# Sums of the weight tiles by transfers that add, and another order of the seven products, in a hybrid-decoder layer

## The chip, the cores and the metric

The kernel runs on one core of a Trainium2 chip. A core has five engines with queues of their own: TensorE (PE, matmuls; its weight loads are shown apart as PEld), VectorE (DVE), ScalarE (ACT), GpSimd (POOL) and SyncE (SP). Each works through its own instructions strictly in order. Transfers are issued on SP's queue (plain ones) and on POOL's (here: those that add what they carry to what lies at their destination). The metric is the device time of one execution, in microseconds; lower is better.

## The reference

One layer on x of 1024 rows by 1024 columns, float32: a norm, a pooling mixer (four causal windows of 2, 4, 8 and 16 rows, a 256x256 matrix for each quarter of the columns), a residual, and a gated ConvFFN, which holds most of the work:

```python
def conv_ffn(x, w_in, conv_w, conv_b, w_out):          # x: 1024 x 1024
    h = causal_depthwise_conv(x @ w_in, conv_w, conv_b)  # w_in: 1024 x 5632
    val, gate = jnp.split(h, 2, axis=-1)
    return (jax.nn.silu(gate) * val) @ w_out             # w_out: 2816 x 1024

x = x + pool_mixer(rms_norm(x, norm_mix_g), pool_w, pool_b, pool_scale)
x = x + conv_ffn(rms_norm(x, norm_ffn_g), ffn_w_in, ffn_conv_w, ffn_conv_b, ffn_w_out)
```

## The kernel before

**Stages.** The mixer comes first (to about 75 us), eight blocks of 128 rows one behind the other. Then the product with w_in, in 22 tiles of 128 + 128 hidden columns (a val and a gate block), to about 468 us, and the product with w_out (the line with `oP`), which fills the rest.

**A tile of w_in.** A tile is one load of 1 MB (`load_in`, SP, tile `win`, two buffers). It holds four quarters, A11, A12, A21 and A22, each 128x512. The normed activations are held as operands of their own: B11, B21, B22 and the combinations T1 to T4. A tile's product is made in seven products and not eight (Winograd's form of Strassen's method), and for that four sums of quarters are needed: S3 = A11 + A21, S1 = A21 + A22 (written over A21), S2 = A11 + S1 (over A11), S4 = A12 + S2 (over A12). The table `STEPS` says which left operand meets which right one, and in which PSUM bank: P1 A11 B11 in X, P6 S2 T2 in Y, P5 S1 T1 in Z, P2 A12 B21 in X, P7 S3 T3 in Y, P3 S4 B22 in Z, P4 A22 T4 in Y. P2 adds onto P1's bank, P3 onto P5's, P7 and P4 onto P6's, and between two products of one bank an engine reads what stands there (`step`): after P1 ScalarE (q1), after P6 VectorE (q2, in the profile `q<-Y`), after P5 VectorE (r), after P7 VectorE (hb).

**A product.** Every left operand is split in a high part (ScalarE's copy, rounded) and the rest (VectorE's subtraction): `split`, named A11s, S1s and so on, seven buffers (`hl`). A product is twelve matmuls of 128x512.

**The end of a tile.** Three-tap convolution of val and gate (ScalarE one wide instruction, VectorE two, for each), Silu on ScalarE, VectorE's product, a store of 512 KB on SP (`g_dram`). It is done by the engines while TensorE is at the next tile.

**What sets the order.** A list `events` of (tile, product) gives TensorE's order; the first two tiles are interleaved with the mixer. At each event the operand of the event five further on is prepared (`prep_in`): its sums, then its split. When a tile's A22 has been prepared, the load of the tile after next is issued into the buffer that it leaves. A list scheduler then merges the engines' streams; what it made of them is shown below.

**Where the sums are made.** For tiles 0 and 1 by transfers: `sums_in` with step 0 loads A11 a second time from memory into a buffer of its own for S3 (SP, 256 KB) and issues two adding transfers of 256 KB on POOL's queue (S3 += A21, then A21 += A22); with step 1 two more (A11 += S1, then A12 += S2). For tiles 2 to 21 `prep_in` makes all four by VectorE, in the helper `add` (line 353 in the profile, `win<-win` and `S<-win`).

**The norm's factors.** `gain_rows` spreads the 1024 factors of the second norm over all partitions with eight matmuls against an identity. The constant `ident` holds its rows turned (even ones first); `woven` reads it with a step of 64, so that the result stands in plain order.

Of the kernel before, what the change touches and what calls it, by code (L numbers as in the profile page):

```python
# [10 lines left out]
AF = mybir.ActivationFunctionType  # L11
# [3 lines left out]
P = 128  # L15
# [4 lines left out]
NK = D // P  # L20
NF = F // P
# [6 lines left out]
FOLD = 2 * D**0.5  # L28
# [22 lines left out]
def woven(t):  # L51
    return t.rearrange("p (a b) -> p b a", a=2)
# [11 lines left out]
def trunk_kernel(ctx: ExitStack, tc: tile.TileContext, x, consts, par, rows, pool_w, w_in, w_out, out):  # L64
    nc = tc.nc
# [14 lines left out]
    def bank2(name):  # L80
        return ps_p.tile([P, 2 * NH], F32, tag="ps", name=name)

    def raw_tile(name):
        return work.tile([P, 2, D], F32, tag="raw", name=name, bufs=2)

    def hl_tile(name):
        return hls.tile([P, 2, NH], F32R, tag="hl", name=name, bufs=7)

    def split(src, name, log=None):
        t = hl_tile(name)  # L90
        nc.scalar.activation(t[:, 0, :], src, AF.Copy)  # L91
        m = nc.vector.tensor_tensor(t[:, 1, :], src, t[:, 0, :].bitcast(F32), ALU.subtract)  # L92
        if log is not None:
            log.append(m.ins)
        return t
# [20 lines left out]
    scale = rows_raw[:, 0, :GRP]  # L116
# [49 lines left out]
    ident = cst[:, ID:]  # L166

    marks = {}
# [27 lines left out]
    def mixer_norm(j):  # L196
        t = bands[j] = pp.tile([P, NG, P], F32, tag="bandr", name=f"bandr{j}", bufs=2)
        for groups in [slice(0, 2), slice(2, 4)] if j == 0 else [slice(0, NG)]:
            marks[f"band{j}"] = normed(t[:, groups, :], (band if j else band0)[:, groups, :], stats[j])
# [46 lines left out]
    def gain_rows():  # L246
        ps = bank2("ps_gain")
        for k in range(NK):
            gain = par_sb[:, GF + k : GF + k + 1].to_broadcast([P, P])
            marks["gain_pe"] = nc.tensor.matmul(ps[:, k * P : (k + 1) * P], gain, woven(ident), start=True, stop=True).ins  # L250
        gain_b = pp.tile([P, D], F32, tag="gain_b", name="gain_b")
        marks["gain"] = nc.scalar.activation(gain_b, ps, AF.Copy, scale=FOLD).ins
        return gain_b

    ds, gains = {}, []
# [6 lines left out]
    def mixer_window(j, ps=None):  # L262
        ps = window_sums(j) if ps is None else ps
        dh = ds[j] = pp.tile([P, NK, P], F32, tag="dh", name=f"dh{j}", bufs=2)
        ps3 = ps.rearrange("p (c s) -> p c s", c=NK)
        first = ps3[:, :, :HALO]
        if j == 0:
            marks["first"] = nc.vector.tensor_tensor(first, first, fac, ALU.mult).ins
        elif j > 1:
            nc.vector.tensor_tensor(first, first, edges[:, :, j * HALO : (j + 1) * HALO], ALU.add)  # L270
        marks[f"dh{j}"] = nc.scalar.activation(dh, ps3, AF.Copy).ins
# [9 lines left out]
    def mixer_out(j, stats=True):  # L281
        dh = ds.pop(j)
        ps = bank2(f"psy{j}")
        for c in range(NK):
            o = ps[:, c // 2 * GRP : (c // 2 + 1) * GRP]
            nc.tensor.matmul(o, dh[:, c, :], wps[:, c, :], start=c % 4 == 0, stop=False, skip_group_check=True)  # L286
        for h in range(2):
            cols = slice(h * NH, (h + 1) * NH)
            m = nc.tensor.matmul(ps[:, cols], ones, bias_hl[:, cols], start=False, stop=True, skip_group_check=True)
        marks[f"psy{j}"] = m.ins  # L290
        x1 = n2s[j] = xs.pop(j)
        marks[j] = nc.vector.tensor_tensor(x1, ps, x1, ALU.add).ins
        nc.sync.dma_start(x1_dram[j * P : (j + 1) * P, :], x1)
        if stats:
            mixer_out_stats(j)
# [4 lines left out]
    def ffn_norm(j):  # L300
        x1, r = n2s[j]
        n2 = n2s[j] = pp.tile([P, D], F32, tag="n2", name=f"n2_{j}", bufs=2)
        nc.vector.tensor_tensor(r[1], r[0], r[1], ALU.mult)
        nc.vector.scalar_tensor_tensor(n2, x1, r[1], gains[0], op0=ALU.mult, op1=ALU.mult)
# [40 lines left out]
    def load_in(n):  # L345
        raws[n] = raw_tile(f"win{n}")
        nc.sync.dma_start(raws[n], w_in[order[n]])
# [4 lines left out]
    def add(out, a, b):  # L352
        nc.vector.tensor_tensor(out, a, b, ALU.add)  # L353

    def tmp(name):
        return work.tile([P, NH], F32, tag="sum", name=name, bufs=3)

    def sums_in(n, step):

        def more(out, a):  # L360
            nc.gpsimd.dma_start(out, a, accum_op=ALU.add)

        a11, a12, a21, a22 = (raws[n][:, i, k * NH : (k + 1) * NH] for i in range(2) for k in range(2))
        if step == 0:
            s3 = sums[n, "S3"] = tmp(f"S3_{n}")
            nc.sync.dma_start(s3, w_in[order[n]][:, 0, :NH])
            more(s3, a21)
            more(a21, a22)
        else:
            sums[n, "S2"] = a11  # L370
            more(a11, a21)
            sums[n, "S4"] = a12
            more(a12, a11)

    def prep_in(n, op):
        a11, a12, a21, a22 = (raws[n][:, i, k * NH : (k + 1) * NH] for i in range(2) for k in range(2))
        if op in ("S1", "S2") and (n, "S3") not in sums:
            s3 = sums[n, "S3"] = tmp(f"S3_{n}")
            add(s3, a11, a21)
            add(a21, a21, a22)  # L380
        if op in ("S2", "S4") and (n, "S2") not in sums:
            sums[n, "S2"] = a11
            add(a11, a21, a11)
        if op == "S4" and (n, "S4") not in sums:
            add(a12, a12, a11)
        if op == "S3":
            src = sums[n, "S3"]
        else:
            src = {"A11": a11, "A12": a12, "S1": a21, "A22": a22, "S2": a11, "S4": a12}[op]
        aops[n, op] = split(src, f"{op}s_{n}")  # L390
        if op == "A22" and n + 2 < NF:
            load_in(n + 2)

    def product(bank, a, b, opens):
        m = 0
        for k in range(4):
            ks = slice(k * P, (k + 1) * P)
            for i, l in ((0, 0), (0, 1), (1, 0)):
                nc.tensor.matmul(bank, a[:, i, ks], woven(b[:, l, k, :]), start=opens and m == 0, stop=m == 11, skip_group_check=not opens)  # L399
                m += 1  # L400

    STEPS = {
        "P1": ("A11", "B11", "X"), "P6": ("S2", "T2", "Y"), "P5": ("S1", "T1", "Z"), "P2": ("A12", "B21", "X"),
        "P7": ("S3", "T3", "Y"), "P3": ("S4", "B22", "Z"), "P4": ("A22", "T4", "Y"),
    }
# [54 lines left out]

    events = [(n, p) for p in ("P1", "P2") for n in range(2)]
    events += [(n, p) for p in ("P5", "P3") for n in range(2)] + [(n, p) for n in range(2) for p in ("P6", "P7", "P4")]
    events += [(n, p) for n in range(2, NF) for p in STEPS]
    LOOK = 5

    def prep_event(k):
        if k < len(events):
            n, p = events[k]
            prep_in(n, STEPS[p][0])

    def event(k):
        if k >= 4:
            prep_event(k + LOOK)
        n, p = events[k]
        step(n, p)
        if p == "P4":
            gated(n)
# [44 lines left out]
    for j in range(2, NS + 4):  # L522
        if 3 < j < NS:
            mixer_norm(j)
        if 1 <= j - 1 < NS and j > 2:
            mixer_window(j - 1, {3: sums2, 4: sums3}.get(j))
        if 1 <= j - 2 < NS:
            with tc.issue_after(marks[f"band{min(j, 4)}"]) if j > 2 else nullcontext(), tc.issue_after(marks["psd3"]):
                mixer_out(j - 2)
        if 0 <= j - 2 < NS:  # L530
            with tc.issue_after(marks["dh1+"]):
                ffn_norm(j - 2)
        if 0 <= j - 4 < NS:
            ffn_operand(j - 4)
        if j in (4, 6):
            load_in(j // 2 - 2)
            sums_in(j // 2 - 2, 0)
        if 5 <= j <= 8:
            with tc.issue_after(marks[j - 2]), tc.issue_after(marks[f"b{j - 3}"]):
                prep_event(j - 5)  # L540
        if j in (7, 8):
            sums_in(j - 7, 1)
        if j in (8, 10, 11):
            event((8, 10, 11).index(j))
        with tc.issue_after(marks["edges"]):
            stat(j + 1)
            stat(j + 2)
# [154 lines left out]
    for k in range(-SLOOK, len(oevents)):  # L702
        p, f = oevents[k + SLOOK] if k + SLOOK < len(oevents) else (None, 0)
# [8 lines left out]
        with tc.issue_after(lasts[-1]) if lasts else nullcontext():  # L712
# [12 lines left out]
            p, f = oevents[k]  # L725
# [27 lines left out]
        for i, g, c, bank in steps:  # L753
            a, b = oops[p, g]
            alone = opens and (p, i) != ("P4", 3)
            for m, (u, v) in enumerate(((0, 0), (0, 1), (1, 0))):
# [3 lines left out]
                    start=opens and first, stop=g == NP2 - 1 and m == 2, skip_group_check=not alone,  # L760
# [83 lines left out]
```

## Time and profile before

| | |
|---|---|
| median of three runs | 673.11 us (672.62 to 673.33) |
| the profiled execution, its own time | 672.94 us |
| its span, first to last instruction | 671.1 us |
| granted TensorE clock | 1.000 |
| busy: PE, DVE, ACT, POOL | 663.3, 591.6, 338.3, 13.1 us |
| bytes moved | 85.49 MB, 127 GB/s on average |

A row of the timeline has its start, its length, engine, line, instruction, tiles (out<-in), count, and in brackets how long the engine sat idle before it and what ended that. A window's row has each engine's busy time in that stretch with the number of instructions, the granted clock, the share of the transfer engines that was busy, and GB/s. Successive instructions of VectorE overlap by some 0.08 us, so one of 0.68 us costs 0.60 of the engine's time in a row of them. "DMA to landing" is the time from a transfer's issue to its arrival.

### The profile page before, as it was taken

The numbers are of one execution on the slowest core, as the hardware profiler recorded it, in microseconds if no ns is written. First come the engines' busy times: TensorE is split into PE (matmuls) and PEld (weight loads), VectorE is DVE, ScalarE is ACT, GpSimd is POOL, SyncE is SP. The second block draws the span as 40 slices with busy tenths as digits, with TensorE's granted clock in tenths as the row PEclk, the third lists the DMA queues.
The fourth block names the chain that finished last, engine by engine and source line by source line (L and its number), as shares of the span: only waits on it lengthen the run. The fifth ranks groups of instructions, "written<-read, shape, count | busy, mean of one in ns | idle before, by whom it ended". The sixth has DMA issues, their size and how long they took to land.

```text
span 671.1 us, 8537 instructions
## 1 busy us (share of the span) xinstructions
PE 663.3 (99%) x3164; PEld 578.5 (86%) x3164; DVE 591.6 (88%) x881; ACT 338.3 (50%) x517; POOL 13.1 (2%) x33
## 2 busy tenths in 40 slices
PE   8999999999999999999999999999999999999998
PEld 7999778888888888888888888888888888888886
DVE  4797999999988888989888888887988988999995
ACT  5696646544455444445454544544554444344441
POOL 3021000000000000000000000000000000000000
PEclk9999999999999999999999999999999999999999
DMA  8883210233211222222222221239999720122231
GB/s 266 294 223 106 84 63 32 100 118 126 84 59 80 95 95 94 95 94 95 95 94 75 83 91 61 101 109 322 347 335 348 278 64 0 55 102 78 65 126 64
DMA packets 32962, 85.49 MB, mean 127 GB/s; under 512 B 3708, under 2 KB 5656, under 8 KB 30104
## 3 DMA queue, kind: packets, MB, share of 16 engines
q1 hardware_dynamic: 31728, 82.83, 34.5%
q0 software_dynamic: 1184, 2.11, 1.9%
q8 instruction: 25, 0.41, 0.3%
q14 instruction: 17, 0.14, 0.1%
q10 hardware_dynamic: 8, 0.00, 0.0%
HBM read 62.89 MB, written 19.92 MB: 123 GB/s over the span
## 4 chain that ended last, share of the span: by engine, by line
PE 75%; DVE 19%; ACT 2%; DMA 2%; issue 1%; SPq 0%; ACTq 0%; DVEq 0%
PE Y L399 22%; PE oP L758 17%; PE X L399 14%; PE Z L399 14%; PE psy L286 4%; DVE oAP L92 3%; DVE oBP L92 3%; PE psd L203 2%; ACT oAP L91 2%; DVE T L339 1%; DVE z L353 1%; DVE blk L350 1%; DVE A12s L350 1%; DVE B21s L350 1%; DMA win<-in_w_in_dram 1%
## 5 line engine op out<-in xcount | busy, mean ns | idle before, releaser
L758 PE MATMUL oP<-oBP,oAP 128*128 128x512 f32 (+1 forms) x924 | 198.9, 378 | 0.1
L758 PEld LDWEIGHTS oP<-oBP,oAP 128*128 128x128 f32 x924 | 174.0, 189 | 25.1 <-DVE oBP L92 0.5
L399 PE MATMUL Z<-T,S1s 128*128 128x512 f32 x264 | 61.2, 380 | 0.6 <-DVE T L339 0.3
L399 PE MATMUL X<-B,A11s 128*128 128x512 f32 x264 | 61.3, 380 | 0.2 <-DVE A11s L92 0.2
L399 PE MATMUL Y<-T,S3s 128*128 128x512 f32 x264 | 60.8, 380 | 0.6 <-DVE q L428 0.6
L399 PE MATMUL Y<-T,S2s 128*128 128x512 f32 x264 | 60.8, 379 | 0.5 <-ACT S2s L91 0.5
L399 PE MATMUL Y<-T,A22s 128*128 128x512 f32 x264 | 60.8, 380 | 0.2 <-DVE hb L436 0.2
L399 PE MATMUL X<-B,A12s 128*128 128x512 f32 x264 | 60.7, 379 | 0.0
L399 PE MATMUL Z<-B,S4s 128*128 128x512 f32 x264 | 60.4, 379 | 0.0
L399 PEld LDWEIGHTS Z<-T,S1s 128*128 128x128 f32 x264 | 49.7, 189 | 8.6 <-DVE T L339 0.7
L399 PEld LDWEIGHTS Y<-T,S3s 128*128 128x128 f32 x264 | 49.7, 189 | 8.3 <-DVE q L428 1.4
L399 PEld LDWEIGHTS Y<-T,S2s 128*128 128x128 f32 x264 | 49.8, 189 | 7.9 <-ACT S2s L91 0.9
L399 PEld LDWEIGHTS Y<-T,A22s 128*128 128x128 f32 x264 | 49.7, 189 | 8.0 <-DVE hb L436 1.0
L399 PEld LDWEIGHTS X<-B,A11s 128*128 128x128 f32 x264 | 49.7, 189 | 7.6 <-DVE A11s L92 0.6
L399 PEld LDWEIGHTS Z<-B,S4s 128*128 128x128 f32 x264 | 49.9, 189 | 7.1
L399 PEld LDWEIGHTS X<-B,A12s 128*128 128x128 f32 x264 | 49.8, 189 | 7.0
L91 ACT ACTIVATE oBP<-blk 128x512 fp32r<-128x512 f32 x53 | 33.1, 625 | 44.2 <-PE oP L758 30.7
L457 ACT ACTIVATE gate<-gate 128x1024 f32<-128x1024 f32 x22 | 23.2, 1056 | 47.4 <-DVE gate L448 47.4
L92 DVE TENSOR_TENSOR oBP<-blk,oBP 128x512 fp32r<-128x512 f32 x53 | 36.5, 688 | 8.6 <-ACT oBP L91 6.6
L91 ACT ACTIVATE oAP<-blk 128x512 fp32r<-128x512 f32 x55 | 34.1, 620 | 19.3 <-DVE blk L350 16.8
L353 DVE TENSOR_TENSOR win<-win 128x512 f32<-128x512 f32 x60 | 41.1, 687 | 1.1
L92 DVE TENSOR_TENSOR oAP<-blk,oAP 128x512 fp32r<-128x512 f32 x55 | 37.7, 685 | 2.6 <-ACT oAP L91 2.6
(132 smaller groups left out, 936.1 us busy)
## 6 DMA issues: line engine op xcount, KB each, us to landing
win<-in_w_in_dram SPq DMA_DIRECT2D x22, 1024.0 KB, 4.9
g_dram<-val SPq DMA_DIRECT2D x22, 512.0 KB, 2.6
blk<-g_dram SPq DMA_DIRECT2D x33, 256.0 KB, 5.2
blk<-in_w_out_dram SPq DMA_DIRECT2D x31, 256.0 KB, 6.0
A12s<-g_dram SPq DMA_DIRECT2D x22, 256.0 KB, 5.0
B21s<-in_w_out_dram SPq DMA_DIRECT2D x22, 256.0 KB, 2.9
x_dram<-x SPq DMA_DIRECT2D x8, 512.0 KB, 2.6
z<-x_dram SPq DMA_DIRECT2D x16, 256.0 KB, 5.2
```

Source lines behind the costliest of these rows:

```text
L91: nc.scalar.activation(t[:, 0, :], src, AF.Copy)
L92: m = nc.vector.tensor_tensor(t[:, 1, :], src, t[:, 0, :].bitcast(F32), ALU.subtract)
L203: m = nc.tensor.matmul(ps[:, c * P : (c + 1) * P], src[:, c * P : (c + 1) * P], weights[:, c // 2, :], start=True, stop=True)
L286: nc.tensor.matmul(o, dh[:, c, :], wps[:, c, :], start=c % 4 == 0, stop=False, skip_group_check=True)
L339: nc.vector.tensor_tensor(l, src, h.bitcast(F32), ALU.subtract)
L350: nc.vector.tensor_tensor(out, a, b, ALU.subtract)
L353: nc.vector.tensor_tensor(out, a, b, ALU.add)
L399: nc.tensor.matmul(bank, a[:, i, ks], woven(b[:, l, k, :]), start=opens and m == 0, stop=m == 11, skip_group_check=not opens)
L457: nc.scalar.activation(gate, gate, AF.Silu)
L758: nc.tensor.matmul(bank, a[:, u, i * P : (i + 1) * P], woven(b[:, v, :])[:, c.start // 2 : c.stop // 2, :], start=opens and first, stop=g ...
```

## The change

From tile 2 on, all four sums are made by transfers. Step 0 of `sums_in` (the second load of A11, S3 and S1) is issued with the tile's load; step 1, now S2 alone, once A11 has been split, since it writes over A11; step 2, S4, once A12 has been split. `prep_in` keeps its VectorE sums in the text, but no tile comes to them any more. The products of a tile stand in the order P1 P5 P6 P2 P7 P3 P4 from tile 2 on (before P1 P6 P5 P2 P7 P3 P4), so that S1 is needed ahead of S2. In `gain_rows` the identity is read plainly, and ScalarE's copy writes its result with a step of two.

```diff
         ps = bank2("ps_gain")
         for k in range(NK):
             gain = par_sb[:, GF + k : GF + k + 1].to_broadcast([P, P])
-            marks["gain_pe"] = nc.tensor.matmul(ps[:, k * P : (k + 1) * P], gain, woven(ident), start=True, stop=True).ins
+            marks["gain_pe"] = nc.tensor.matmul(ps[:, k * P : (k + 1) * P], gain, ident, start=True, stop=True).ins
         gain_b = pp.tile([P, D], F32, tag="gain_b", name="gain_b")
-        marks["gain"] = nc.scalar.activation(gain_b, ps, AF.Copy, scale=FOLD).ins
+        marks["gain"] = nc.scalar.activation(
+            gain_b.rearrange("p (k s a) -> p k a s", k=NK, a=2), ps.rearrange("p (k a s) -> p k a s", k=NK, a=2), AF.Copy, scale=FOLD
+        ).ins
...
             nc.sync.dma_start(s3, w_in[order[n]][:, 0, :NH])
             more(s3, a21)
             more(a21, a22)
-        else:
+        elif step == 1:
             sums[n, "S2"] = a11
             more(a11, a21)
+        else:
             sums[n, "S4"] = a12
             more(a12, a11)
...
         aops[n, op] = split(src, f"{op}s_{n}")
+        if n >= 2 and op == "A11":
+            sums_in(n, 1)
+        if n >= 2 and op == "A12":
+            sums_in(n, 2)
         if op == "A22" and n + 2 < NF:
             load_in(n + 2)
+            sums_in(n + 2, 0)
...
-    events += [(n, p) for n in range(2, NF) for p in STEPS]
+    events += [(n, p) for n in range(2, NF) for p in ("P1", "P5", "P6", "P2", "P7", "P3", "P4")]
...
         if j in (7, 8):
             sums_in(j - 7, 1)
+            sums_in(j - 7, 2)
```

**POOL's queue.** Before, these are the last transfers on it, those of tiles 0 and 1 (`S3_0` and `S3_1` are the buffers of S3, `win0` and `win1` the tiles):

```order
L361 DMA S3_0_427<-win0_425 128x512
L361 DMA win0_425<-win0_425 128x512
L361 DMA S3_1_552<-win1_550 128x512
L361 DMA win0_425<-win0_425 128x512
L361 DMA win1_550<-win1_550 128x512 x2
L361 DMA win0_425<-win0_425 128x512
L361 DMA win1_550<-win1_550 128x512
```

In the change they go on to tile 21; here from S2 of tile 10 on. The rows are, in turn, S2 of tile 10; S3 and S1 of tile 11; S4 of tile 10; S2 of tile 11; S3 and S1 of tile 12:

```order
L363 DMA win10_1907<-win10_1907 128x512
L363 DMA S3_11_2048<-win11_2046 128x512
L363 DMA win11_2046<-win11_2046 128x512
L363 DMA win10_1907<-win10_1907 128x512
L363 DMA win11_2046<-win11_2046 128x512
L363 DMA S3_12_2187<-win12_2185 128x512
L363 DMA win12_2185<-win12_2185 128x512
```

S4 of a tile stands behind S3 and S1 of the next. S3's transfer waits for that next tile's load, and S1's, which writes over what S3's reads, waits until S3's has landed. This holds for tiles 2, 3 and 5 to 20; for tile 4 S4 stands between S3 and S1 of tile 5.

**VectorE, a tile in the middle.** Before, from q2 of tile 10 (the rows of line 353 are S2 of tile 11, S3 and S1 of tile 12, S4 of tile 11):

```order
L428 TENSOR_TENSOR q2_10_2187<-Y10_2174,q1_10_2167 128x512
L353 TENSOR_TENSOR win11_2034<-win11_2034 128x512
L458 TENSOR_TENSOR val15_2139<-val15_2139,gate37_2143 128x1024
L433 TENSOR_TENSOR r_10_2205<-q1_10_2167,Z10_2192 128x512
L92 TENSOR_TENSOR S2s_11_2211<-win11_2034,S2s_11_2211 128x512
L92 TENSOR_TENSOR S1s_11_2228<-win11_2034,S1s_11_2228 128x512
L353 TENSOR_TENSOR S3_12_2345<-win12_2172 128x512
L353 TENSOR_TENSOR win12_2172<-win12_2172 128x512
L92 TENSOR_TENSOR A12s_11_2245<-win11_2034,A12s_11_2245 128x512
L353 TENSOR_TENSOR win11_2034<-win11_2034 128x512
```

In the change, from q2 of tile 10 to the split of A22 of tile 11:

```order
L436 TENSOR_TENSOR q2_10_2223<-Y10_2210,q1_10_2180 128x512
L92 TENSOR_TENSOR S2s_11_2242<-win11_2046,S2s_11_2242 128x512
L92 TENSOR_TENSOR A12s_11_2259<-win11_2046,A12s_11_2259 128x512
L444 TENSOR_TENSOR hb10_2257<-r_10_2204,Y10_2210 128x512
L92 TENSOR_TENSOR S3s_11_2276<-S3_11_2048,S3s_11_2276 128x512
L447 TENSOR_TENSOR ha10_2240<-Z10_2191,q2_10_2223 128x512
L92 TENSOR_TENSOR S4s_11_2303<-win11_2046,S4s_11_2303 128x512
L455 SCALAR_TENSOR_TENSOR val5_2292<-ha10_2240,par_sb_126,val5_2292 128x1023
L449 TENSOR_TENSOR hb10_2257<-q1_10_2180,Y10_2210 128x512
L456 SCALAR_TENSOR_TENSOR val5_2292<-ha10_2240,par_sb_126,val5_2292 128x1022
L92 TENSOR_TENSOR A22s_11_2321<-win11_2046,A22s_11_2321 128x512
```

The four sums are gone. Behind A22's split there follow, as before, the two instructions of the gate's convolution with A11's split between them, then r, S1's split, the product with the gate (all three ahead of q2 now) and q2 of the tile. Between S4's split and A22's stand the same three instructions as before.

**ScalarE at tile 2.** Before, from its first split (`T4` is a right operand that P4 of tile 0 needs):

```order
L91 ACTIVATE A11s_2_935<-win2_847 128x512
L338 ACTIVATE T4_792<-n2f_154 128x1024 x2
L446 ACTIVATE val0_972<-ha0_776,par_sb_126 128x1024
L425 ACTIVATE ha1_820<-X1_735 128x512
L91 ACTIVATE S2s_2_956<-win2_847 128x512
L91 ACTIVATE S1s_2_983<-win2_847 128x512
```

In the change:

```order
L91 ACTIVATE A11s_2_943<-win2_847 128x512
L91 ACTIVATE S1s_2_961<-win2_847 128x512
L340 ACTIVATE T4_792<-n2f_154 128x1024 x2
L454 ACTIVATE val0_977<-ha0_776,par_sb_126 128x1024
L91 ACTIVATE S2s_2_988<-win2_847 128x512
```

S1's split of tile 2, which waits for S1's transfer, now stands ahead of T4. On VectorE nine instructions that stood ahead of A22's split of tile 2 no longer do: its four sums are gone, and three evictions and two instructions of the gate's convolution stand behind it.

## The prediction, made before the changed kernel was run

> **What bounds the kernel now.** I read the page's busy times first, then busy time by stage, then TensorE's own rows in order of time.
>
> ```profile
> PE 663.3 (99%) x3164; PEld 578.5 (86%) x3164; DVE 591.6 (88%) x881; ACT 338.3 (50%) x517; POOL 13.1 (2%) x33
> ...
> 100.00:120.00 20.00, 19.48 (x89) 16.25 (x87) 19.99 (x27) 12.15 (x16) 0.00 (x0) 1.00 0.15 53
> 120.00:140.00 20.00, 19.46 (x89) 16.75 (x90) 19.21 (x28) 10.57 (x16) 0.00 (x0) 1.00 0.35 132
> 180.00:200.00 20.00, 20.00 (x95) 17.50 (x94) 18.00 (x24) 10.42 (x15) 0.00 (x0) 1.00 0.21 79
> ...
> 133.33 2.86 PE L399 MATMUL Y<-T,S3s 128*128 128x512 f32 x12 [0.41 <-DVE q L428]
> ...
> 410.83 2.75 PE L399 MATMUL Y<-T,A22s 128*128 128x512 f32 x12
> 413.42 2.75 PE L399 MATMUL X<-B,A11s 128*128 128x512 f32 x12
> ...
> 467.81 2.54 PE L758 MATMUL oP<-oBP,oAP 128*128 128x512 f32 x11
> ```
>
> TensorE (PE) is the bound: from 140 on it never idles, and VectorE (DVE), at 18.0 of 20, just keeps up. One product of twelve matmuls takes 413.42 - 410.83 = 2.59 us, so a tile of seven takes **18.13 us**. Only between 100 and 140, where VectorE is full (19.99), does TensorE miss 0.52 + 0.54 = 1.06 us. That, at most 2 us with the refilling of its pipeline, is all that a freer VectorE can return.
>
> **The change part by part.** *The sums.* Eighty adds leave VectorE:
>
> ```profile
> L353 DVE TENSOR_TENSOR win<-win 128x512 f32<-128x512 f32 x60 | 41.1, 687 | 1.1
> L353 DVE TENSOR_TENSOR S<-win 128x512 f32<-128x512 f32 x20 | 13.7, 684 | 0.8 <-DMA win<-in_w_in_dram 0.8
> ```
>
> That is 54.8 us, 2.7 us a tile, of an engine that does not set the end after 140: worth nothing there. In their place stand 80 transfers that add, on POOL's queue, one behind the other. Their price is in the rows of tiles 0 and 1, which do it so already. Behind each of these four POOL issues stands its own time to landing, between them two SP rows that fall beside them, and last the least, median and greatest of all eight:
>
> ```profile
> 28.08 0.89 POOL L361 DMA_DIRECT2D S<-win  x1 [21.10 <-DMA S<-in_w_in_dram]
> DMA to landing us min/median/max: 7.6/7.6/7.6
> 28.69 0.37 SPq L347 DMA_DIRECT2D win<-in_w_in_dram  x1
> 36.16 0.87 POOL L361 DMA_DIRECT2D win<-win  x1 [7.19 <-DMA win<-in_w_in_dram]
> DMA to landing us min/median/max: 4.9/4.9/4.9
> 38.37 0.86 POOL L361 DMA_DIRECT2D S<-win  x1 [1.33 <-PE pst L319]
> DMA to landing us min/median/max: 4.0/4.0/4.0
> 39.45 26.75 SPq L293 DMA_DIRECT2D x_dram<-x  x5
> 42.94 0.86 POOL L361 DMA_DIRECT2D win<-win  x1 [0.51 <-issue]
> DMA to landing us min/median/max: 3.5/3.5/3.5
> ...
> DMA to landing us min/median/max: 3.3/3.4/7.6
> ```
>
> An add takes 3.3 us at best, 0.86 of it on POOL. The one at 38.37, with a 512 KB store issued 1.1 us behind it, takes 4.0; the one at 42.94, behind another add, 3.5. When POOL waits for an add to land it starts about 0.5 us later: 28.08 + 7.6 = 35.68 against 36.16, and 38.37 + 4.0 = 42.37 against 42.94.
>
> *The loop that this closes.* Take A22(n) as VectorE's half of the split of A22 of tile n, the last reader of that tile's buffer. In the order shown above, S4's add of tile n+1 stands on POOL behind both adds of tile n+2, whose load waits for A22(n). And A22(n+1) stands on VectorE behind S4's split. So each A22 waits for the one before it through load, add, add's issue, add. The pieces on SP, ScalarE (ACT) and VectorE, from a tile in the steady stretch:
>
> ```profile
> 211.60 0.63 ACT L91 ACTIVATE S4s<-win 128x512 fp32r<-128x512 f32 x1 [1.96 <-PE Z L399]
> 212.38 1.24 ACT L446 ACTIVATE val<-ha,par_sb 128x1024 f32<-128x1024 f32 x1
> 213.65 1.28 DVE L447 SCALAR_TENSOR_TENSOR val<-ha,par_sb,val 128x1023 f32<-128x1023 f32 x1 [0.69 <-ACT val L446]
> 214.85 0.68 DVE L441 TENSOR_TENSOR hb<-q,Y 128x512 f32<-128x512 f32 x1
> 215.45 1.28 DVE L448 SCALAR_TENSOR_TENSOR val<-ha,par_sb,val 128x1022 f32<-128x1022 f32 x1
> 216.64 0.68 DVE L92 TENSOR_TENSOR A22s<-win,A22s 128x512 fp32r<-128x512 f32 x1
> 217.35 0.33 SPq L347 DMA_DIRECT2D win<-in_w_in_dram  x1
> ...
> 199.23 0.33 SPq L347 DMA_DIRECT2D win<-in_w_in_dram  x1
> ...
> win<-in_w_in_dram SPq DMA_DIRECT2D x22, 1024.0 KB, 4.9
> ```
>
> A22's end to the load's issue 0.03 (216.64 + 0.68 against 217.35); the load 4.9; POOL's start 0.5; S3's add 4.0 (the value of the row at 38.37, since the 512 KB store of val also falls here: it is issued six instructions of VectorE, some 5.4 us, behind A22, as this add is); POOL's start 0.5; the issue of S1's add 0.86; S4's add, which follows an add, 3.5; then S4's split on ScalarE 0.63, val behind it 1.24, and on VectorE val 1.20, hb 0.60, val 1.19, A22 0.68, together 5.54. The sum is 0.03 + 4.9 + 0.5 + 4.0 + 0.5 + 0.86 + 3.5 + 5.54 = **19.8 us against the 18.13** that TensorE needs: 1.7 us too long, in every tile. With everything at its least (load 4.9, both adds 3.3) it is 18.9, still above. With the adds at 4.9, the row at 36.16, it is 22.1. I take 19.8, whose terms have the nearest neighbours.
>
> The Trainium skill, page "DMA: Bandwidth & Descriptors", section "Anatomy of one DMA", gives such a transfer 2.0 us plus its bytes by 436 GB/s. By it an add of 256 KB is an estimated 2.6 us and the loop 4.9 + 2 x 2.6 + 7.4 = 17.5 us, below TensorE's. Eight adds measured here at 3.3 or more speak against it.
>
> TensorE meets the delay where P7 of a tile may not write the Y bank before VectorE has read P6 out of it (q, the reader that row 133.33 shows it waiting for). After A22 stand six more instructions and then q: three wide of about 1.2 and three narrow of 0.6 behind it, 6.0 us with q. P6 and P7 now have one product between them and not two; while VectorE is on time that costs nothing, since q takes 0.7 of 2.59.
>
> *The start.* SP's load at 117.10 marks A22(2) now:
>
> ```profile
> 79.32 7.91 SPq L347 DMA_DIRECT2D win<-in_w_in_dram  x2
> DMA to landing us min/median/max: 5.5/5.5/5.5
> ...
> 90.31 1.06 ACT L338 ACTIVATE T<-n2f 128x1024 fp32r<-128x1024 f32 x1 [2.97 <-DVE n2f L575]
> 92.53 2.35 DVE L339 TENSOR_TENSOR T<-n2f,T 128x1024 fp32r<-128x1024 f32 x2
> 117.10 0.33 SPq L347 DMA_DIRECT2D win<-in_w_in_dram  x1
> 132.70 0.33 SPq L347 DMA_DIRECT2D win<-in_w_in_dram  x1
> ```
>
> Of what VectorE does before A22(2), four adds go and three narrow and two wide instructions now stand behind it: 4 x 0.6 + 3 x 0.6 + 2 x 1.2 = 6.6 us earlier, 110.5. But ScalarE now has S1's split of tile 2 ahead of T4, and that waits for an add: load 79.32 + 5.5 = 84.8, S3's add from 85.3 to 88.6, S1's from 89.1, while the load of tile 3 (issued near 87) fills the queues, so 4.0 to 4.9: about 93.5. T4's hi parts start at 94 and not at 90.31, VectorE's lo parts 2.5 us later than 92.53. A22(2) ends near **113**.
>
> *The sum.* A22(3) one loop later, 132.8. Tile 4's S4 stands on POOL ahead of the next S1, so its way is shorter by an add and a start: 0.03 + 4.9 + 0.5 + 0.86 + 3.5 + 5.54 = 15.3 us, what VectorE needed between 117.10 and 132.70 too: A22(4) at 148.1. Sixteen loops to A22(20): 148.1 + 16 x 19.8 = 464.9. P7 of tile 20 starts 6.0 later, 470.9; with it ten products are left, 25.9 us, and the second half starts at 496.8 instead of 467.81: **+29 us**. The second half, 203 us of unbroken matmuls, stays. The profiled execution took 672.94 us round its span of 671.1, next to the median of 673.11: 672.9 + 29 = **702 us**.
>
> *The factors.* Eight products (sixteen passes) with the identity read in order:
>
> ```profile
> 9.13 2.35 PE L250 MATMUL ps_gain<-cst,par_sb 128*128 128x128 f32 x16
> 11.32 1.95 PE L203 MATMUL psd<-bandr,x 128*128 128x128 f32 x16
> 13.84 1.06 ACT L180 ACTIVATE junk_a<-x 128x1024 bf16<-128x1024 f32 x1 [1.30 <-DMA x<-in_x_dram]
> 18.07 0.55 DVE L189 TENSOR_SCALAR edge_band<-cst,st_e 128x512 f32<-128x512 bf16 x1
> ```
>
> At best 0.4 us (the next line's pitch), taken back by 18.6, where the edges wait for edge_band. The copy that now writes every second element has 1.3 us of ScalarE idle behind it. Both cost nothing; if that cover were gone, 0.4 less or 1 us more.
>
> **The rivals.** *One: the relief decides, and the kernel is faster.* If the two adds land in 5.8 us together (18.13 less the loop's other 12.3), the loop hides behind TensorE; the 1.1 to 2 us between 100 and 140 come back: 671 to 672. For it: a VectorE full there. Against it: no add was under 3.3, and T4's new wait takes 2.5 us from that very stretch. *Two: no change, 673.* The same short loop, but the wait ahead of T4 eats the relief. This is where the page's 2.6 us would lead. *Three: much slower.* Each tile now moves 1 MB in, 0.5 MB out, 0.25 MB of S3 and four adds. An add that shares its time with a load took 7.6 (28.08, with the load at 28.69 beside it). Should S3's or S4's add meet a load so, the loop is 12.3 + 7.6 + 3.5 = 23.4 us, and the time 702 + 17 x 3.6 = 763; it decides from a loop of 21.6 on. Against it: the loop itself puts the load ahead of both. *That the change doesn't do what it says*: the rows show the adds gone from VectorE, so no.
>
> **How the numbers follow.** Forecast 0.78; rival one 0.07, two 0.06, three 0.09. A difference of 0.2%, 1.35 us, is about what can be told here. Faster 0.07, same 0.06, slower 0.87. Each microsecond of the loop counts seventeen-fold: at 18.9 the time is 686, at 21.6 733. Below 683 lie rivals one and two and little else, above 733 rival three: the range is 683 to 733.
>
> **What would show it.** Right: TensorE waiting at P7's Y bank for q, once a tile; loads of the weight tiles 19 to 21 us apart after 170, where now they are 18.1; ScalarE idle before S4's split, released by POOL; POOL idle before S1's add, released by its own S3's add; adds of 3.3 to 5 us. Wrong: TensorE without gaps from 140 on and loads 18.1 apart (then the adds are cheaper, or S4's add isn't held by its neighbours), or VectorE's adds still there. If the loads stand 22 us or more apart, it was the sharing, rival three.

## The result, and the profile after

The changed kernel takes **744.62 us** (median of 4; 743.78 to 745.11) against 672.87 us (672.44 to 673.33) of the kernel before, measured beside it: a ratio of 1.106, 95% interval 1.1047 to 1.1074. The forecast was 702 us, in a range of 683 to 733. The sign was right, the size was not: of 72 us that were lost, 29 were forecast. The profiled execution of the changed kernel took 745.11 us round a span of 743.3.

From its page: the span, the busy times, the chain of waits, three of the groups (the idle time before them behind the second bar), and two rows of transfers (KB each, median us to landing):

```profile
span 743.3 us, 8859 instructions
...
PE 683.3 (92%) x3164; PEld 585.5 (79%) x3164; DVE 545.8 (73%) x801; ACT 331.0 (45%) x517; POOL 82.5 (11%) x113
...
DMA 26%; PE 18%; DVE 17%; issue 15%; ACT 4%; POOL 2%; SPq 0%; POOLq 0%; ACTq 0%; DVEq 0%
...
L407 PE MATMUL Y<-T,S3s 128*128 128x512 f32 x264 | 74.5, 441 | 47.5 <-DVE q L436 47.4
...
L92 DVE TENSOR_TENSOR S4s<-win,S4s 128x512 fp32r<-128x512 f32 x22 | 15.1, 692 | 75.1 <-ACT S4s L91 75.1
...
L91 ACT ACTIVATE S4s<-win 128x512 fp32r<-128x512 f32 x22 | 13.9, 630 | 114.0 <-DMA win<-win 109.4
...
win<-win POOLq DMA_DIRECT2D x66, 256.0 KB, 4.3
...
S<-win POOLq DMA_DIRECT2D x22, 256.0 KB, 4.2
```

VectorE is 46 us less busy (eighty adds, 0.57 us each), and TensorE falls from 99% to 92%. TensorE waits at P7 for q (47.4 us), VectorE for ScalarE's half of S4's split, and ScalarE for S4's add (109.4 us). Transfers now hold the first place in the chain.

The places of the sum, from the timeline of the same execution: SP's load behind A22(2), A22(3), A22(4) and A22(19), and the first product of the second half:

```profile
114.18 0.33 SPq L349 DMA_DIRECT2D win<-in_w_in_dram  x1
...
135.77 0.33 SPq L349 DMA_DIRECT2D win<-in_w_in_dram  x1
...
154.85 0.33 SPq L349 DMA_DIRECT2D win<-in_w_in_dram  x1
...
484.50 0.33 SPq L349 DMA_DIRECT2D win<-in_w_in_dram  x1
...
539.84 5.34 PE L767 MATMUL oP<-oBP,oAP 128*128 128x512 f32 x24
```

From 154.85 to 484.50 there are fifteen loops of **21.98 us** in the mean; 19.8 was forecast, TensorE needs 18.13. The second half starts at 539.84, not at 496.8, and takes 203.5 us, as before (671.1 - 467.81 = 203.3).

One loop in order of time, the longest of the fifteen; behind each row of POOL its time to landing (in the second the first of the two is S1's add with 5.8, the second, S4's, with 7.5):

```profile
265.85 0.33 SPq L349 DMA_DIRECT2D win<-in_w_in_dram  x1
270.89 0.86 POOL L363 DMA_DIRECT2D S<-win  x1 [2.12 <-DMA win<-in_w_in_dram]
DMA to landing us min/median/max: 4.4/4.4/4.4
271.25 0.33 SPq L467 DMA_DIRECT2D g_dram<-val  x1
275.81 1.75 POOL L363 DMA_DIRECT2D win<-win  x2 [4.06 <-DMA S<-win]
DMA to landing us min/median/max: 5.8/6.6/7.5
276.15 0.33 SPq L368 DMA_DIRECT2D S<-in_w_in_dram  x1
283.93 0.64 ACT L91 ACTIVATE S4s<-win 128x512 fp32r<-128x512 f32 x1 [8.53 <-DMA win<-win]
289.43 0.33 SPq L349 DMA_DIRECT2D win<-in_w_in_dram  x1
```

This is the loop that the prediction drew, link by link. Its pieces, as means over the fifteen loops, beside the terms of the forecast:

| piece of the loop | forecast | measured |
|---|---|---|
| load's issue to the start of S3's add | 5.43 | 5.47 |
| S3's add, and POOL's start behind it | 4.50 | 4.88 |
| S1's issue to S4's split (in it S4's add) | 4.36 | **6.12** |
| S4's split to the next load | 5.54 | 5.50 |
| loop | 19.83 | 21.97 |

Three pieces come within 0.4 us; S4's add does not. Of the 2.14 us that the loop is too long, 1.76 are in that row. POOL issues S4's add 0.54 us behind S1's, and in fourteen of the fifteen loops SP issues S3's plain load of the tile after close to it, from 2.4 us ahead to 1.7 us behind. The add takes 4.3 to 7.5 us (median 5.3, mean 5.5), where 3.5 had been put in.

### The profile page after: what moved, and what is told of

It is laid out like the page before. It is cut to its first block, busy times and chain, and to the rows that moved or that the text cites. A ratio compares the mean times of both kernels' runs of the same rounds, so it can differ in the third digit from the quotient of the medians.

```text
span 743.3 us, 8859 instructions
## 1 busy us (share of the span) xinstructions
PE 683.3 (92%) x3164; PEld 585.5 (79%) x3164; DVE 545.8 (73%) x801; ACT 331.0 (45%) x517; POOL 82.5 (11%) x113
## 4 chain that ended last, share of the span: by engine, by line
DMA 26%; PE 18%; DVE 17%; issue 15%; ACT 4%; POOL 2%; SPq 0%; POOLq 0%; ACTq 0%; DVEq 0%
PE oP L767 15%; DMA win<-win 13%; DMA win<-in_w_in_dram 7%; DMA S<-win 5%; DVE oAP L92 3%; DVE oBP L92 3%; DVE val L455 2%; ACT val L454 2%; DVE val L456 2%; ACT oAP L91 2%; PE Y L407 2%; POOL win L363 1%; DVE hb L449 1%; DVE z L355 1%; DVE blk L352 1%
## 5 line engine op out<-in xcount | busy, mean ns | idle before, releaser
L407 PE MATMUL Y<-T,S3s 128*128 128x512 f32 x264 | 74.5, 441 | 47.5 <-DVE q L436 47.4
L407 PEld LDWEIGHTS Y<-T,S3s 128*128 128x128 f32 x264 | 56.2, 219 | 65.3 <-DVE q L436 56.0
L363 POOL DMA_DIRECT2D win<-win x66 | 57.3, 952 | 339.0 <-DVE A11s L92 224.2
L92 DVE TENSOR_TENSOR S4s<-win,S4s 128x512 fp32r<-128x512 f32 x22 | 15.1, 692 | 75.1 <-ACT S4s L91 75.1
L91 ACT ACTIVATE S4s<-win 128x512 fp32r<-128x512 f32 x22 | 13.9, 630 | 114.0 <-DMA win<-win 109.4
```

## Experiments

**The loop, or the sharing, or the order of the products**

*S4's add ahead of both adds of the next tile.* All sums stay transfers; the adds of S3 and S1 of tile n + 1 stand behind S4's of tile n in POOL's queue (`issue_after` puts what its block issues behind the named instruction, here S4's add, on the same engine):

```diff
             nc.sync.dma_start(s3, w_in[order[n]][:, 0, :NH])
-            more(s3, a21)
-            more(a21, a22)
+            if n < 4:
+                sums_in(n, 3)
+        elif step == 3:
+            more(sums[n, "S3"], a21)
+            more(a21, a22)
...
         if n >= 2 and op == "A12":
             sums_in(n, 2)
+            if 3 <= n < NF - 1:
+                with tc.issue_after(marks["S4"]):
+                    sums_in(n + 1, 3)
```

> All four sums stay transfers; only POOL's order is changed, from tile 4 on: S4's add of a tile stands ahead of S3's and S1's of the next. Theory, the loop through POOL's queue: S4 no longer waits for the next tile's load. What is left is a shorter loop, from A22 over the split of A11 (1.8 us), S2's add (0.3 + 4.1), the splits of S2 and A12 (2.4), S4's add (0.2 + 4.2 to 5.2) and the 5.5 us behind S4's split: 18.6 to 19.6 us against 21.98 now. Seventeen times 2.4 to 3.4 us come back: 687 to 704 us, and up to 5 less if the start gains too. Rival, the transfers share the engines: as many bytes are moved, so 735 to 745 us. Rival, the order of the products: no change, 744 us.

Measured: 685.35 us, ratio 1.0195 (1.0178 to 1.0212). Of 72 us lost, 59 are back with no transfer fewer. Two rows of POOL from its timeline, S4's add with its landing, and S3's of the next tile behind it:

```profile
254.50 0.86 POOL L363 DMA_DIRECT2D win<-win  x1 [5.73 <-DVE A12s L92]
DMA to landing us min/median/max: 3.3/3.3/3.3
255.04 1.21 POOL L363 DMA_DIRECT2D S<-win  x1
```

The loop through POOL's queue is shown, and the other two theories fall: the same bytes in the same order of products. Tiles stand 18.2 us apart. POOL now waits for A12's split, as expected, but S4's add, going first, takes 3.3 to 3.7 and not 4.2 to 5.2, so this shorter loop hardly exceeds TensorE's 18.13. Most of the 13 us left are stalls of TensorE before 165 (1.97, 0.53, 2.68 and 1.43 us, two of them at a lower clock afterwards).

*S4's add ahead of S1's alone.* S3's add keeps its place:

```diff
             nc.sync.dma_start(s3, w_in[order[n]][:, 0, :NH])
             more(s3, a21)
-            more(a21, a22)
+            if n < 4:
+                sums_in(n, 3)
+        elif step == 3:
+            more(a21, a22)
```

> As the run before, but S3's add stays ahead of S4's and only S1's stands behind it. Theory, the loop: S4 waits for the load and S3's issue but not for S3's landing. By the load that is 5.45 + 0.9 + 5.2 + 5.5 = 17 us, so the loop over S2's add (18.6 to 19.6) decides here too: 687 to 704 us. If S4's add and S3's add lengthen each other the way S1's and S4's do now, up to 712. Rival, sharing alone: 735 to 745 us.

Measured: 684.86 us in one execution, tiles 18.3 us apart. So the wait for S3's landing, with S1's issue behind it, closes the long loop; the load and S3's issue may stand ahead of S4's add.

*The order of the products alone*, in the kernel before:

```diff
-    events += [(n, p) for n in range(2, NF) for p in STEPS]
+    events += [(n, p) for n in range(2, NF) for p in ("P1", "P5", "P6", "P2", "P7", "P3", "P4")]
```

> The kernel before with nothing but the new order of the products from tile 2 on; all sums of these tiles by VectorE. Theory, the loop: the order by itself costs nothing while VectorE is on time, 671 to 676 us. Rival, the order (P6 and P7 of one bank with one product between them): TensorE waits for q in every tile, 1 to 2 us, so 690 to 715 us.

Measured: 674.04 us, ratio 1.0032 (1.0019 to 1.0046). Tiles stand 18.13 us apart from 164 on, so in the steady stretch the order is free. What it costs is one stall, in tile 2, where VectorE is full:

```profile
116.70 2.64 PE L399 MATMUL Z<-B,S4s 128*128 128x512 f32 x11 [2.98 <-DVE r L433]
```

*The identity alone*, in the kernel before:

```diff
-            marks["gain_pe"] = nc.tensor.matmul(ps[:, k * P : (k + 1) * P], gain, woven(ident), start=True, stop=True).ins
+            marks["gain_pe"] = nc.tensor.matmul(ps[:, k * P : (k + 1) * P], gain, ident, start=True, stop=True).ins
...
-        marks["gain"] = nc.scalar.activation(gain_b, ps, AF.Copy, scale=FOLD).ins
+        marks["gain"] = nc.scalar.activation(
+            gain_b.rearrange("p (k s a) -> p k a s", k=NK, a=2), ps.rearrange("p (k a s) -> p k a s", k=NK, a=2), AF.Copy, scale=FOLD
+        ).ins
```

> The kernel before with nothing but the plain identity and the copy that writes with a step. Forecast and theory: no difference, 672.5 to 673.5 us, within 0.2%. Rival: the copy with a step is slower and lies on the way, 674 us or more.

Measured: 672.88 us, ratio 0.9996 (0.9987 to 1.0005). No difference.

**What lengthens S4's add**

*S3's plain load twice.*

```diff
-            nc.sync.dma_start(s3, w_in[order[n]][:, 0, :NH])
+            for _ in range(2 if n >= 4 else 1):
+                nc.sync.dma_start(s3, w_in[order[n]][:, 0, :NH])
```

> The changed kernel, with S3's plain load of 256 KB issued twice from tile 4 on (the second writes the same again); it falls beside S1's and S4's adds. S4's add, issued 0.54 us behind S1's, takes 5.4 us there and 3.3 to 3.6 where it goes first. Theory, the two adds of one queue lengthen each other and the load has no part: 742 to 748 us, S4's add 5.2 to 5.5. Rival, all that moves shares: S4's add 6 us or more, a loop of 22.6 to 23.2 us, 755 to 765 us.

Measured: 742.38 us in one execution, S4's add 5.5 in the mean. This tells little, and the row of SP says why: the two issues span 3.98 us. The second starts when the first has landed, 3 to 4.5 us behind it, and in nine of fourteen loops it lies beside no more than the last 2 us of S4's add.

```profile
249.26 3.98 SPq L369 DMA_DIRECT2D S<-in_w_in_dram  x2
```

*S3's plain load left out.*

```diff
-            nc.sync.dma_start(s3, w_in[order[n]][:, 0, :NH])
+            if n < 5:
+                nc.sync.dma_start(s3, w_in[order[n]][:, 0, :NH])
+            else:
+                nc.vector.memset(s3, 0.0)
```

> The changed kernel without S3's plain load from tile 5 on: VectorE clears the buffer instead, so S3 is A21 alone there and the result is another. Theory, the two adds lengthen each other: S4's add still 5.2 to 5.5, 740 to 746 us. Rival, the load beside them shares: S4's add 4.0 to 4.6, a loop of 21.1 us, 724 to 732 us.

Measured: 728.33 us in one execution, a loop of 21.01 us. In most loops S1's add lands after 3.3 and S4's after 4.3; one such pair with its least, median and greatest landing:

```profile
288.00 1.75 POOL L363 DMA_DIRECT2D win<-win  x2 [3.99 <-DMA S<-win]
DMA to landing us min/median/max: 3.3/3.8/4.3
```

The rival was right here: the load has a part, about 1 us. But the add is still 1 us longer than one alone, so the pair has a part too.

*S1's add cut in two*, the greater part behind S4's (step 3 is called as in the first experiment, S4's add is set behind the first part):

```diff
             more(s3, a21)
-            more(a21, a22)
+            if n < 4:
+                more(a21, a22)
+            else:
+                marks["S1", n] = more(a21[:, :64], a22[:, :64])
+        elif step == 3:
+            more(a21[:, 64:], a22[:, 64:])
```

> The changed kernel, with S1's add (256 KB) cut from tile 4 on: its first 64 columns keep the old place and the wait for S3's landing, S4's add of the tile before follows at once, and the other 448 columns of S1 stand behind S4's. The loop through the queue is kept as it was; only the bytes of S1 that are under way beside S4's add are pushed behind it. Theory, S4's add is long because it follows a whole add by 0.54 us: it falls from 5.4 to 3.3 to 3.7, the loop to 5.45 + 4.9 + 0.6 + 3.4 + 0.1 + 5.5 = 19.9 us (what was forecast as 19.8), and 744 to 744 - 17 x 2.0 = 710 us; 704 to 714. Rival, S3's plain load beside S4's add is all of it: S4's add stays above 5, 740 us or more.

Measured: 729.37 us in one execution, a loop of 20.91 us; S4's add takes 4.46 us in the mean. Both sides missed: half of the gap closes. That the other half is the load's is for the next run to show.

*Both edits together.*

> The changed kernel with both of the edits that each took about 1 us from S4's add: S1's add cut in two as in the run of 729 us, and S3's plain load left out from tile 5 on (VectorE clears the buffer, S3 is A21 alone, the result is another) as in the run of 728 us. Theory, S4's add is lengthened by two neighbours, and each adds its own microsecond: alone it takes 3.3 to 3.6, the loop is 5.45 + 4.9 + 0.6 + 3.4 + 0.1 + 5.5 = 19.9 us, as forecast for the change, and the time 744.6 - 17 x 2.05 = 710; 706 to 714 us. Rival, one cause seen twice (whichever of the two is taken away, the other no longer matters): S4's add 4.2 or more, 722 to 728 us.

Measured: 716.82 us in one execution, a loop of 20.21 us. S4's add, the second of three issues, takes 3.7 us nearly always (the first, of 32 KB, 2.2). The row is the first issue, and below it stand the landings of these two:

```profile
284.54 0.86 POOL L363 DMA_DIRECT2D win<-win  x1 [3.59 <-DMA S<-win]
DMA to landing us min/median/max: 2.2/2.9/3.7
```

Side by side (means over fifteen loops each):

| kernel | S4's add | loop | time |
|---|---|---|---|
| the change | 5.5 | 21.98 | 744.6 |
| without S3's load | 4.5 | 21.01 | 728.3 |
| S1's add in two | 4.46 | 20.91 | 729.4 |
| both | 3.8 | 20.21 | 716.8 |

One edit takes 1.0 us, the other 1.0, both 1.7: nearly their sum, and the rival, one cause seen twice, falls. The medians (5.3, 4.3, 4.3 and 3.7 us) say the same. The time is 3 us above the upper end that was expected, since the add did not come quite down to 3.4 and S3's add stayed at 4.5. From the first row to the last the loop loses 1.77 us and the time 27.8: each microsecond counts some sixteen-fold.

The trace of the change itself bears out the load's part. In two of its loops SP issued S3's plain load 1.5 us or more ahead of S4's add, and there the add takes 4.3 us, as it does without the load; in the other loops it takes 4.8 or more. One of the two, S1's and S4's adds again in one row:

```profile
321.04 0.33 SPq L368 DMA_DIRECT2D S<-in_w_in_dram  x1
322.93 1.75 POOL L363 DMA_DIRECT2D win<-win  x2 [6.28 <-DMA S<-win]
DMA to landing us min/median/max: 3.3/3.8/4.3
```

**Where transfers cost nothing, and whether they gain anything**

*S4 alone by VectorE.*

```diff
-        if n >= 2 and op == "A12":
-            sums_in(n, 2)
```

> S3, S1 and S2 by transfers, S4 alone by VectorE (20 adds of 0.69 us). Theory, the loop: no transfer stands between a load and S4 any more; A22 to A22 takes 1.8 + 4.4 + 2.4 + 0.7 + 5.5 = 14.8 us, less than TensorE's 18.13, so TensorE is the bound again from 140 on: 671 to 674 us, and a tile every 18.13 us. Rival, sharing: three quarters of the adds are still there, so 715 to 730 us.

Measured: 679.01 us, ratio 1.0092 (1.0077 to 1.0107), above the 671 to 674 expected. The steady part came as the theory has it (18.13 us a tile), so the rival, as many bytes as cause enough, is refuted again. What is lost lies ahead of it, in two stalls of TensorE at products of tile 2, each followed by half clock in this trace (the last two rows are loads of the steady part):

```profile
97.10 0.94 PE L405 MATMUL X<-B,A11s 128*128 128x512 f32 x2 [2.11 <-DVE A11s L92]
...
124.62 4.54 PE L405 MATMUL Y<-T,A22s 128*128 128x512 f32 x12 [2.86 <-DVE hb L442]
...
404.10 0.33 SPq L349 DMA_DIRECT2D win<-in_w_in_dram  x1
422.23 0.33 SPq L349 DMA_DIRECT2D win<-in_w_in_dram  x1
```

*The same from tile 4 on*, tiles 2 and 3 as before:

```diff
-        if n >= 2 and op == "A11":
+        if n >= 4 and op == "A11":
             sums_in(n, 1)
...
             load_in(n + 2)
-            sums_in(n + 2, 0)
+            if n >= 2:
+                sums_in(n + 2, 0)
...
+    events += [(n, p) for n in range(2, 4) for p in STEPS]
-    events += [(n, p) for n in range(2, NF) for p in ("P1", "P5", "P6", "P2", "P7", "P3", "P4")]
+    events += [(n, p) for n in range(4, NF) for p in ("P1", "P5", "P6", "P2", "P7", "P3", "P4")]
```

> S3, S1 and S2 by transfers and S4 by VectorE as in the run that took 679 us, but only from tile 4 on; tiles 2 and 3 as in the kernel before, sums by VectorE and the old order of products. Theory: all of what that run lost against the kernel before lies in tiles 2 and 3 (S1's split of tile 2 ahead of T4; VectorE held by S2's split of tile 3), so 671 to 673 us. Rival, the transfers cost something in every tile: 676 to 679 us.

Measured: 676.88 us, ratio 1.0064 (1.0051 to 1.0076). The number is the rival's, the mechanism is not: tiles stand 18.13 us apart from 184 on, and most of the loss is one stall, moved to the first tile with transfers:

```profile
153.76 2.86 PE L406 MATMUL Y<-T,S3s 128*128 128x512 f32 x12 [2.37 <-DVE q L435]
```

*All four by transfers, S4's add ahead, and A12 split before S2.* On top of the first experiment:

```diff
             n, p = events[k]
+            if n >= 2:
+                p = {"P6": "P2", "P2": "P6"}.get(p, p)
             prep_in(n, STEPS[p][0])
```

> All four sums by transfers from tile 2 on, S4's add ahead of the next tile's, as in the run that took 685 us; beside that A12 is split ahead of S2, so that S4's add needs no longer wait for it. Theory: what was left there is the loop A11, S2's add, splits of S2 and A12, S4's add; without the splits between the adds it is 1.8 + 0.3 + 4.1 + 0.5 + 3.4 + 0.1 + 5.5 = 15.7 us, below TensorE's 18.13: 677 to 680 us, the start's loss alone. Rival, transfers that share: still 683 us or more, tiles up to 19 us apart.

Measured: 674.64 us, ratio 1.0027 (1.0015 to 1.0039). Its busy times from the page, then, from its timeline, the stall that was left and two loads of the steady part:

```profile
PE 662.8 (99%) x3164; PEld 578.4 (86%) x3164; DVE 543.6 (81%) x801; ACT 340.7 (51%) x517; POOL 82.5 (12%) x113
```

```profile
97.70 0.70 PE L413 MATMUL X<-B,A11s 128*128 128x512 f32 x2 [2.23 <-DVE A11s L92]
...
200.83 0.33 SPq L349 DMA_DIRECT2D win<-in_w_in_dram  x1
218.96 0.33 SPq L349 DMA_DIRECT2D win<-in_w_in_dram  x1
```

This is the change with its order mended: every transfer is still there, TensorE is the bound at 99%, VectorE is 48 us less busy, and nothing is gained by it.

*The same with S1's split of tile 2 behind T4's* on ScalarE (`marks["hi"]` is ScalarE's half of T4's split):

```diff
-            prep_in(n, STEPS[p][0])
+            with tc.issue_after(marks["hi"]) if (n, p) == (2, "P5") else nullcontext():
+                prep_in(n, STEPS[p][0])
```

> As the run with S4's add ahead and A12 split first (674.64 us), and S1's split of tile 2 placed behind T4's on ScalarE. Theory, what that run lost is the start: TensorE's 2.23 us at the first product of tile 2, since T4 waits for S1's add there. With it gone 672 to 673.5 us, no difference to the kernel before within 0.2%; VectorE's 55 us less bring nothing, since TensorE sets the end. Rival, the relief between 100 and 140 counts: 671.5 us or less. Rival, the loss comes from elsewhere: 674.5 us still.

Measured: 674.99 us, ratio 1.0029 (1.0017 to 1.0041): the second rival. The stall at 97.70 is gone and another of the same size stands 11 us later. By the rows it goes back to S2's add of tile 2, the second of a pair on POOL (ScalarE idle 4.92 us before S2's split); no run was made to take this wait away:

```profile
100.34 0.63 ACT L91 ACTIVATE S2s<-win 128x512 fp32r<-128x512 f32 x1 [4.92 <-DMA win<-win]
...
108.59 1.89 PE L413 MATMUL Y<-T,A22s 128*128 128x512 f32 x4 [2.31 <-DVE hb L450]
```

No version tried beats the kernel before.

## Why the prediction was right in sign and wrong in size

**The bound: right.** TensorE set the end before; with 48 us taken off VectorE and no loop in the way the time is 674.6, not less.

**The loop: right.** Load, S3's add, S1's issue, S4's add, S4's split, A22, load: each link stands in the rows above, and putting S4's add first removes it. TensorE meets it where forecast, at P7's bank behind q, 20 times, 47.4 us.

**The price of S4's add: this step failed.** The prediction took 3.5 us "behind another add", from the row at 42.94. The add before that one, which its lines leave out, was issued 1.36 us ahead of it:

```profile
41.58 0.85 POOL L361 DMA_DIRECT2D win<-win  x1 [2.35 <-DVE st_b L185]
DMA to landing us min/median/max: 3.3/3.3/3.3
```

That add landed at 44.9, the one at 42.94 at 46.4, 1.5 us later. In the loop S4's add is issued only 0.54 us behind S1's, since nothing makes it wait; in the run without S3's load the pair at 288.00 lands at 291.3 and 292.8, again 1.5 us apart. With that distance between the landings, an add issued 1.36 us behind the other takes 3.5 us, and one issued 0.54 us behind it takes 4.3. So the row was right and the distance between the issues was not carried over. S3's plain load, which also falls beside S4's add, was not in the sum at all. The runs put about 1 us on each of the two neighbours. So S4's add took 5.5 us and not 3.5, and S1's issue 0.54 and not 0.86 (that is the length of POOL's row, not the distance to the next): the term of 4.36 us was 6.12, sixteen times over.

S3's add was better placed (4.0 beside the store of val forecast, 4.4 measured in the mean). Its longest times have a neighbour that nobody listed. The page has 25 packets, 0.41 MB, on a queue for instructions:

```profile
q8 instruction: 25, 0.41, 0.2%
```

By the times of the packets in the trace one of them, 16 KB, moved beside each of the three longest of S3's adds in the loops (5.0, 5.9 and 6.6 us; the other twelve took 3.3 to 4.6) and of the two longest of S4's (6.9 and 7.5). Beside two more of S4's one moved in their last microsecond. In the run without S3's load the three longest of S3's adds (5.8 to 6.0 us) have such a neighbour too. The traces show only that these fall together; no run was made to test it.

**The start: a wait was missed.** A22(2) came at 114.2 (113 forecast) and A22(3) 21.6 us later, the longer loop again. A22(4) was to follow in 15.3 us, as tile 4's S4 stands ahead of S1 on POOL; it took 19.1. Of these 3.8 us 1.1 are S4's add once more (4.5 us to landing), and 2.7 a wait ahead of it. Four rows of that stretch:

```profile
142.10 0.63 ACT L91 ACTIVATE S2s<-win 128x512 fp32r<-128x512 f32 x1 [4.05 <-DMA win<-win]
...
143.11 0.62 ACT L91 ACTIVATE A12s<-win 128x512 fp32r<-128x512 f32 x1
...
143.76 0.69 DVE L92 TENSOR_TENSOR A12s<-win,A12s 128x512 fp32r<-128x512 f32 x1 [0.31 <-ACT A12s L91]
...
144.75 1.75 POOL L363 DMA_DIRECT2D win<-win  x2 [2.88 <-DMA S<-win]
```

S4's add writes over A12 and starts 0.3 us after A12's split ends at 144.45; that split stands behind S2's, and S2's waits for S2's add. (The row names S3's landing, also near 144.5; S4's add needs no such wait.) Where A12 is split first, this step takes 17.3 us (146.44 - 129.17, the loads behind A22(3) and A22(4)), against 19.6 in the first experiment, from which that run differs by this alone. This second loop was not in the prediction; in the change it decides for one tile, in the first two experiments it is the one that is left.

**The sum.** A22(4) is 154.85 - 148.1 = 6.8 us late, sixteen loops to A22(20) add 16 x (21.98 - 19.8) = 34.9, together 41.7 of the 43.0 us by which the second half starts later than forecast. What the other 1.3 are was not traced.

**The rivals.** One and two needed a loop below 18.13 us, which came only with another order on POOL, or with S4's sum on VectorE. Behind the second stood the rule of the Trainium skill, page "DMA: Bandwidth & Descriptors", section "Anatomy of one DMA", by which an add of 256 KB is an estimated 2.6 us; none of the 88 in this trace took under 3.2. Rival three named the right kind of cause, adds that share with other transfers, but the wrong neighbour: it feared the load of 1 MB, which was out of the way as the prediction said, while an add and a load of 256 KB each were enough. Its mark for the verdict, loads 22 us apart, was met almost exactly (21.98), with a smaller price per neighbour than its 7.6 us. So a cause of this kind, given a chance of 0.09, decided the size.

**The order and the factors.** The order was called free "while VectorE is on time". That holds in the steady part; in tile 2 VectorE was not on time, by the prediction's own window from 100 to 120, and it costs 0.3%. The factors cost nothing, as forecast.

## What to carry to other kernels

A price taken from a row of the trace carries its neighbours with it: see how far ahead the transfer before it was issued, and list everything that will be under way beside the one being priced. Before an operation is moved to an in-order queue, write down for each entry what it waits for and who stands behind it; here the order of two entries was worth 59 us, and the same transfers, once out of the loop, cost next to nothing (674.6 against 673.0 us). Relief of an engine that is not the bound stays worth nothing even when it is delivered in full.

## What the runs showed of the hardware

**The granted clock can fall after stalls of two to three microseconds.** The kernel before runs at 1.00 throughout, the changed one at 0.981 in the mean. Two stalls of 3.18 us at P7 in its timeline, and then the windows of the 3 us behind each (the clock is the third figure from the end):

```profile
295.46 4.54 PE L407 MATMUL Y<-T,S3s 128*128 128x512 f32 x12 [3.18 <-DVE q L436]
382.53 2.86 PE L407 MATMUL Y<-T,S3s 128*128 128x512 f32 x12 [3.18 <-DVE q L436]
```

```profile
295.46:298.46 3.00, 3.00 (x7) 2.44 (x8) 1.39 (x2) 1.64 (x3) 0.26 (x1) 0.51 0.95 261
382.53:385.53 3.00, 3.00 (x14) 2.65 (x15) 1.49 (x3) 1.74 (x4) 0.00 (x0) 1.00 0.98 265
```

Of the 14 stalls of 2.1 us or more in this trace between 76 and 540, 8 were followed by some 3.3 us at half clock, 1.7 us lost; of the 7 between 1.2 and 1.8 us none. The same length can go either way, so the length alone does not decide. In the changed kernel nothing of the loss is attributed to it: the seven of the fifteen loops that hold a half-clock product take 21.9 us in the mean, the other eight 22.1. Where TensorE is the bound it does count: of the ten executions with the order alone, the six at a clock of 0.999 or more took 673.2 to 674.1 us, the four at 0.995 to 0.997 took 675.5 to 677.0. The Trainium skill, page "TensorE: Matmul & The Clock Gate", section "HAM oscillation — how this bites in real kernels", puts the limit at idle gaps above about 3.4 us; here 2.1 sufficed at times. Its section "What's actually happening" has the gate watch a window that runs on regardless of the kernel, which fits one length with two outcomes.

**An adding transfer is slow by its bytes, too.** With no add issued just ahead, 32 KB land after 2.2 us (S1's first part in the run with both edits) and 256 KB after 3.3: 1.1 us for 224 KB, some 210 GB/s. The second of two adds issued 0.54 us apart takes 1 us longer (4.3 against 3.3 in the run without S3's load), while the first is not slowed.
